# Rotating images by 90 degrees: which rows of the last group are stored first, and for which load the first store waits

## The chip, the core and the metric

The kernel runs on one core of a Trainium2 chip. It uses the vector engine (DVE), the scalar engine (ACT) and the core's 16 DMA engines; all transfers are issued from one queue, that of the sync engine (SP). The metric is the time of one execution on the device in microseconds.

## The reference

```python
batch, c, h, w = 32, 3, 256, 256                      # x is float32
np.rot90(x, k=-1, axes=(-2, -1)).astype(np.float32)
```

Each of the 96 images of 256 x 256 is turned clockwise by a quarter. Nothing is calculated: every element is read once and written once, 25.17 MB in and 25.17 MB out.

## The kernel before

**Tiles.** The input is seen as 24576 rows of 256 floats. A *slab* is 2048 rows (8 images): 128 partitions with 16 rows each, which is 16 KB per partition (`E` = 4096 floats; `Q` = 2048 is half of that, 8 rows; `W` = 256 is one row). The 12 slabs are taken in four groups of 2, 2, 4 and 4 slabs (`sizes`, L39). Each group has one tile in SBUF, `groups[n]`, called u0 to u3, which holds the whole group: it is loaded there, turned in place with the help of some spare tiles, and stored from there. So all tiles are in SBUF at once, no tile is used twice, and no load waits for a store.

**Loads** (L55 to L69). All are issued on SP's queue at the start, in the order of the groups. For the groups 1 to 3 the load `i` of `I` fills every `I`-th partition (`to[i::I]`), in two halves per partition (`a`). In the last group a half is 32 KB, that is two slabs, and a load covers 32 partitions. The last load of all is issued as two: the first half (L66, 1 MB, kept as `mark`) and the second half (L67, 1 MB).

**The turn.** DVE transposes blocks of 32 x 32 (`turn`, L82), and strided patterns on both sides put every element at its place. For a group of four slabs the work is cut in eight: two halves `t`, and four quadrants, A to D, by the halves (`low`, `high`) of the rows and columns. A transposition `move(t, c, r)` (L107) writes into all four slabs of its tile, in the other half `t`; with `c = low` it writes into the lower 8 rows (the lower 8 KB) of each slab's 16, with `c = high` into the upper 8. Two of the eight parts have to be kept aside first: ACT copies one in (L157), DVE transposes the other into the tiles `most` and `rest` (`leave`, L161 and L162). The order of the last group is: the moves D, C and B for both `t` (L164 to L166), ACT's copies of the kept part into the slabs 0, 2, 1, 3 (`enter`, L167 to L170), and last of all DVE's transposition of the part kept by ACT (L171), which writes with `c = low` and `r = low`.

**Order.** `keep` (L73) fixes the order of the instructions on DVE and on ACT as written. The waits between engines and transfers are not written out; the framework derives them from which parts of a tile each instruction and each transfer reads and writes.

**Stores** (L174 to L190). Also on SP's queue, in the order of the groups. Each group is stored in two parts, the even and the odd partitions (`a::2`, 64 partitions each); of each slab a partition's 16 KB go to 16 KB of the output. The very first store is told to wait for `mark` (L178), so that stores do not go into the queue ahead of the loads. In the last group the even partitions are stored in three pieces: slab 0's upper 8 KB, slab 0's lower 8 KB (both L189, 512 KB each), and then the slabs 1 to 3 (L190, 3 MB); the odd partitions follow in one piece of 4 MB (L190).

Of the kernel before, what the change touches and what calls it, by code (L numbers as in the profile page):

```python
# [9 lines left out]
def kernel(  # L10
# [14 lines left out]
    nc = tc.nc  # L25
    fp32 = mybir.dt.float32

    B, C, H, W = x.shape
    P = nc.NUM_PARTITIONS
    R = 16  # L30
    E = R * W
    Q = E // 2
# [8 lines left out]
    groups = [  # L41
        ctx.enter_context(tc.tile_pool(name=f"group{n}", bufs=1)).tile([P, s, E], fp32, name=f"u{n}")
        for n, s in enumerate(sizes)
    ]
# [6 lines left out]
    def rows_of(rows, n):  # L51
        return rows[first[n] * P * R : (first[n] + sizes[n]) * P * R]


    ld = rows_of(rows_in, 0).rearrange("(s i p r) w -> s i p (r w)", s=2, i=2, p=P)  # L55
# [4 lines left out]
    for n in range(1, len(sizes)):  # L60
        I = sizes[n]
        ld = rows_of(rows_in, n).rearrange("(a i m r) w -> i m a (r w)", a=2, i=I, m=P // I)
        to = groups[n].rearrange("p s f -> p (s f)").rearrange("p (a f) -> p a f", a=2)
        for i in range(I):
            if (n, i) == (len(sizes) - 1, I - 1):
                mark = nc.sync.dma_start(out=to[i::I, 0], in_=ld[i][:, 0])  # L66
                nc.sync.dma_start(out=to[i::I, 1], in_=ld[i][:, 1])  # L67
            else:
                nc.sync.dma_start(out=to[i::I], in_=ld[i])  # L69
# [61 lines left out]
    u = groups[0]  # L131
# [42 lines left out]
    st = rows_of(rows_out, 0).rearrange("(s i m r) w -> i m s (r w)", s=2, i=2, m=P // 2)  # L174
# [5 lines left out]
    for n in range(1, len(sizes)):  # L180
        I = sizes[n]
        st = rows_of(rows_out, n).rearrange("(a i m r) w -> a m i (r w)", a=2, i=I, m=P // 2)
        for a in range(2):
            done = 0
            if (n, a) == (len(sizes) - 1, 0):

                done = 1
                for f in (slice(Q, E), slice(0, Q)):
                    nc.sync.dma_start(out=st[a][:, 0, f], in_=groups[n][a::2, 0, f])  # L189
            nc.sync.dma_start(out=st[a][:, done:], in_=groups[n][a::2, done:])  # L190


# [28 lines left out]
```

## Time and profile before

| | |
|---|---|
| Median of 3 runs | 123.51 us (123.16 to 123.54) |
| The profiled execution's own time | 123.7 us |
| Its span in the profile | 121.9 us |
| DVE busy | 86.6 us, 71% of the span |
| ACT busy | 29.1 us, 24% |
| DMA queue | 50.33 MB, 97.2% of 16 engines' span |
| First store issued | at 59.40 us |
| Last transposition of the last group | 96.03 to 99.64 us |
| First store of the last group issued | at 99.71 us |

Positions in time count from the start of the span. A transfer has an issue (the time that SP's queue needs to hand it over) and, later, its packets on the 16 DMA engines; each DMA engine works through its packets in the order in which they were issued. In the profile, an issue row has the issue alone; GB/s and the DMA share come from the packets, each counted where it starts. A packet of 16 KB takes 0.61 us on its engine, so in windows of a quarter of a microsecond the rate jumps; an empty stretch of more than 0.6 us is an idle queue all the same.

### The profile page before, as it was taken

Reading aid. Unit: us, or ns where it says so; the run is one execution under the profiler, and the core shown is the slowest. Engines: PE = TensorE matmul, PEld = TensorE weight load, DVE = VectorE, ACT = ScalarE, POOL = GpSimd, SP = SyncE. Lnnn points to the kernel's source line nnn. Section 1 sums busy time; section 2 is a strip of 40 time slices with the busy share of each in tenths; the row PEclk is TensorE's granted clock in tenths of the full one; section 3 lists DMA queues with packets and bytes.
Section 4 is the critical chain, followed back from the end, with each engine's and each line's share of the span. In section 5 each row is a group of like instructions: output and inputs, shape, how many; then the busy total and the mean of one; then the engine's idle time right before and its main releaser. Section 6 shows DMA issues by size and latency. Waiting matters only on the chain.

```text
span 121.9 us, 135 instructions
## 1 busy us (share of the span) xinstructions
DVE 86.6 (71%) x25; ACT 29.1 (24%) x20; POOL 0.2 (0%) x4
## 2 busy tenths in 40 slices
DVE  0039999999994199999999999999999960000000
ACT  0000400470005199409462194000003400000000
POOL 0000000000000000000000000000000000000000
DMA  3999999997979898989899999999999989999994
GB/s 86 427 430 427 435 430 430 430 516 344 516 344 516 355 505 376 484 387 473 382 430 430 419 425 414 425 430 430 430 430 430 430 344 430 430 425 425 430 430 183
DMA packets 3264, 50.33 MB, mean 413 GB/s; under 512 B 384, under 2 KB 384, under 8 KB 384
## 3 DMA queue, kind: packets, MB, share of 16 engines
q1 hardware_dynamic: 3264, 50.33, 97.2%
HBM read 25.17 MB, written 25.17 MB: 413 GB/s over the span
## 4 chain that ended last, share of the span: by engine, by line
DVE 44%; DMA 34%; issue 3%; DVEq 0%
DMA u<-in_x_dram 34%; DVE u L82 34%; DVE spare L82 6%; DVE most L82 3%; DVE extra L82 2%; DVEq L82 0%
## 5 line engine op out<-in xcount | busy, mean ns | idle before, releaser
L82 DVE STREAM_TRANSPOSE u<-u 128x2048 f32<-128x2048 f32 x16 | 59.7, 3811 | 0.3
L82 DVE STREAM_TRANSPOSE spare<-u 128x2048 f32<-128x2048 f32 (+1 forms) x4 | 11.9, 2995 | 12.7 <-DMA u<-in_x_dram 12.7
L85 ACT COPY u<-spare 128x512 f32<-128x512 f32 (+2 forms) x8 | 10.5, 1347 | 18.6 <-DVE u L82 13.8
L85 ACT COPY u<-extra 128x1024 f32<-128x1024 f32 (+1 forms) x3 | 5.7, 1937 | 11.1 <-DVE u L82 11.1
L85 ACT COPY u<-most 128x448 f32<-128x448 f32 x4 | 2.1, 563 | 20.4 <-DVE u L82 20.4
L85 ACT COPY spare<-u 128x1024 f32<-128x1024 f32 (+1 forms) x3 | 5.7, 1887 | 2.6 <-DMA u<-in_x_dram 2.6
L85 ACT COPY extra<-u 128x2048 f32<-128x2048 f32 x1 | 4.2, 4234 | 2.5 <-issue 2.5
L85 ACT ACT_TABLE_LOAD x1 | 1.3, 1283 | 13.1 <-DMA u<-in_x_dram 13.1
L82 DVE STREAM_TRANSPOSE extra<-u 128x2048 f32<-128x2048 f32 x1 | 3.9, 3920 | 0.0
L82 DVE STREAM_TRANSPOSE most<-u 128x1792 f32<-128x1792 f32 x1 | 3.6, 3634 | 0.0
L82 DVE STREAM_TRANSPOSE u<-spare 128x2048 f32<-128x2048 f32 x1 | 3.6, 3607 | 0.0
L82 DVE STREAM_TRANSPOSE spare<-spare 128x2048 f32<-128x2048 f32 x1 | 2.3, 2330 | 0.0
L82 DVE STREAM_TRANSPOSE extra<-extra 128x2048 f32<-128x2048 f32 x1 | 2.3, 2311 | 0.0
L205 POOL MEMSET const-bfloat16-1.0<- 128x1 bf16 x1 | 0.1, 101 | 0.0
L205 POOL MEMSET const-uint8-127<- 128x1 uint8 x1 | 0.1, 101 | 0.0
L205 POOL MEMSET const-float32-0.0<- 128x1 f32 x1 | 0.1, 98 | 0.2 <-issue 0.2
L205 POOL MEMSET const-float32-1.0<- 128x1 f32 x1 | 0.1, 98 | 0.0
## 6 DMA issues: line engine op xcount, KB each, us to landing
u<-in_x_dram SPq DMA_DIRECT2D x10, 2048.0 KB, 30.4
out_dram<-u SPq DMA_DIRECT2D x3, 4096.0 KB, 19.4
out_dram<-u SPq DMA_DIRECT2D x4, 2048.0 KB, 13.3
u<-in_x_dram SPq DMA_DIRECT2D x4, 1024.0 KB, 20.4
out_dram<-u SPq DMA_DIRECT2D x1, 3072.0 KB, 10.5
out_dram<-u SPq DMA_DIRECT2D x2, 512.0 KB, 3.3
```

The costliest lines, as they stand in the source:

```text
L82: keep(nc.vector.transpose(out=out, in_=in_))
L85: keep(nc.scalar.copy(out=out, in_=in_))
L205: nc = _bacc.Bacc("TRN2", target_bir_lowering=False, num_devices=1)
```

## The change

```diff
         for i in range(I):
             if (n, i) == (len(sizes) - 1, I - 1):
-                mark = nc.sync.dma_start(out=to[i::I, 0], in_=ld[i][:, 0])
+                part = I * E // 2 * 11 // 16
+                mark = nc.sync.dma_start(out=to[i::I, 0, :part], in_=ld[i][:, 0, :part])
+                nc.sync.dma_start(out=to[i::I, 0, part:], in_=ld[i][:, 0, part:])
                 nc.sync.dma_start(out=to[i::I, 1], in_=ld[i][:, 1])
...
         for a in range(2):
-            done = 0
+            u = groups[n][a::2]
             if (n, a) == (len(sizes) - 1, 0):
 
-                done = 1
-                for f in (slice(Q, E), slice(0, Q)):
-                    nc.sync.dma_start(out=st[a][:, 0, f], in_=groups[n][a::2, 0, f])
-            nc.sync.dma_start(out=st[a][:, done:], in_=groups[n][a::2, done:])
+                end = Q + 2 * W
+                nc.sync.dma_start(out=st[a][:, I - 1, end:], in_=u[:, I - 1, end:])
+                nc.sync.dma_start(out=st[a][:, : I - 1], in_=u[:, : I - 1])
+                nc.sync.dma_start(out=st[a][:, I - 1, :end], in_=u[:, I - 1, :end])
+            else:
+                nc.sync.dma_start(out=st[a], in_=u)
```

The change has two parts. The first half of the last load, 32 KB in each of 32 partitions, is issued as two loads, of 22 KB (704 KB in all) and 10 KB (320 KB); `mark`, for which the first store waits, is the one of 22 KB. And the even partitions of the last group are stored in three other pieces: first the upper 6 KB (rows 10 to 15) of slab 3, 384 KB; then the slabs 0 to 2, 3 MB; then the lower 10 KB of slab 3, 640 KB. The odd partitions follow in one piece of 4 MB as before. DVE's and ACT's instructions are the same.

## The prediction

> **What bounds the kernel now.** I read the page's slices first, then the DMA issues, then what the sync queue (SP) waited for, then the last 30 us in order of time, then quarter-microsecond windows. The slices say that the transfers are the bound:
>
> ```profile
> DVE  0039999999994199999999999999999960000000
> ACT  0000400470005199409462194000003400000000
> ...
> DMA  3999999997979898989899999999999989999994
> GB/s 86 427 430 427 435 430 430 430 516 344 516 344 516 355 505 376 484 387 473 382 430 430 419 425 414 425 430 430 430 430 430 430 344 430 430 425 425 430 430 183
> ...
> q1 hardware_dynamic: 3264, 50.33, 97.2%
> ```
>
> Each slice is 3.05 us. DVE has nothing left after slice 33, and DMA is at 8 or 9 tenths all along: 50.33 MB at 430 GB/s are 117.0 of the 121.9 us. (516 beside 344 is an effect of long packets, counted where they start; such a pair has the usual mean.) One slice stands alone: number 33, from 97.5 to 100.6 us, at 344 GB/s between two of 430. The page's chain of waits stops at DVE's last transposition, because stores are all that follows; so the end has to be followed in the transfers themselves. There the next two views matter, the order of time and the windows (DMA share and GB/s are the last two columns):
>
> ```profile
> 88.62 7.37 DVE L82 STREAM_TRANSPOSE u<-u 128x2048 f32<-128x2048 f32 x2
> 92.28 1.03 ACT L85 COPY u<-most 128x448 f32<-128x448 f32 x2 [17.64 <-DVE u L82]
> 96.03 3.61 DVE L82 STREAM_TRANSPOSE u<-spare 128x2048 f32<-128x2048 f32 x1
> 96.03 1.03 ACT L85 COPY u<-most 128x448 f32<-128x448 f32 x2 [2.71 <-DVE u L82]
> ...
> 99.71 1.13 SPq L189 DMA_DIRECT2D out_dram<-u  x2
> 100.89 1.99 SPq L190 DMA_DIRECT2D out_dram<-u  x2
> ```
>
> ```profile
> 99.50:99.75 0.25, 0.13 (x1) 0.00 (x0) 0.00 (x0) 1.00 1.39 590
> 99.75:100.00 0.25, 0.00 (x0) 0.00 (x0) 0.00 (x0) 1.00 0.00 0
> 100.00:100.25 0.25, 0.00 (x0) 0.00 (x0) 0.00 (x0) 1.00 0.04 0
> 100.25:100.50 0.25, 0.00 (x0) 0.00 (x0) 0.00 (x0) 1.00 0.00 0
> 100.50:100.75 0.25, 0.00 (x0) 0.00 (x0) 0.00 (x0) 1.00 0.00 0
> 100.75:101.00 0.25, 0.00 (x0) 0.00 (x0) 0.00 (x0) 1.00 1.18 492
> ```
>
> The last group's first store is issued at 99.71, when the last transposition is over. The stores of the group before run out meanwhile. In the trace's packet records their last packets end between 100.05 and 100.25 on the 16 DMA engines, and the first packets of the last group begin between 100.86 and 101.01: 0.78 us of idle time as the mean of 16. No other stretch has an idle engine for over 0.13 us between 1.8 us (first data) and 120.6 (last). So the gap is all that an ordering of transfers can win; it is 0.6% of the time.
>
> **The change, part by part.** *The 6 KB.* SP waits before L189:
>
> ```profile
> SPq L189 <- DVE u L82: 22.9, 1, 22.9
> SPq L216 <- DMA out_dram<-u: 18.0, 3, 9.7
> ```
>
> That wait ended with the last transposition. It writes only the lower 8 KB (low `c`) of each slab's 16 KB; the upper 8 KB were done at 95.99 (88.62 + 7.37). So in the kernel before, the upper half of slab 0 was held 3.7 us for nothing: what orders the waits takes the strided write too coarsely. In floats of a partition, that write begins at 24 (slab 0) and ends at 14335 (slab 3, row 7); the upper half of slab 0, 2048 to 4095, lies between its ends. The 6 KB of the change are 14848 to 16383, behind its last element. If spans decide, the new store waits for 95.99 only, or for ACT's copies (done at 97.32). Both are before 100.05 by more than 2 us.
>
> Then the sum is this. 6 KB from 64 partitions are 384 KB, 24 KB per DMA engine; a 16 KB packet took 0.614 us, so they last 0.92 us and the engines run dry at 100.97 to 101.17, mean 101.06. The next store (three slabs, 3 MB) can be issued at 99.71, as the first one was. The store issued then took 0.49 us to issue and its first packet came 1.15 us after the start of the issue, 0.66 after its end. The same 3 MB shape took 0.72 us to issue at 100.89. Counted from the end of the issue, its first packet comes at 99.71 + 0.72 + 0.66 = 101.09; from the start, at 100.86. What is left of the gap is 0.12 us at most, some 0.04 as a mean. The gain is 0.78 - 0.04 = 0.74. The 10 KB piece and the last 4 MB are issued behind it while 3 MB (7.3 us) run, so even the slow issues of the trace (1.2 to 1.4 us) are covered there.
>
> *The count and size of pieces.* Stores: 10 before and 10 after, with as many runs (64 + 64 + 192 in the first half of the group). Loads: 14 become 15. Two more packets per engine: 8 KB took 0.309 us and 16 KB 0.614, so a cut costs 2 x 0.309 - 0.614 = 0.004 us, twice, and one more completion record of 0.009. Together 0.02 us, on the path, since the queue is the bound. Runs of 6, 10 and 22 KB are not in the trace. From below they cost nothing; from above, the slowest 8 KB packets (0.345 where 0.309 is usual, 12%) on the 2 MB concerned, 4.9 us, would cost 0.6 us. I take nothing: 8 KB and 16 KB rows differ by 1%.
>
> Here a rule of the Trainium skill speaks against cutting. "DMA: Bandwidth & Descriptors", section Bandwidth, asks for 1 MiB or more per transfer, and its section Anatomy of one DMA (written for another issuing path than this kernel's) puts a fixed 2.0 us on each; charged to the one added piece, that would be an estimated 125.5 us. The trace's two 512 KB stores of L189 follow one another at 1.25 us each, 420 GB/s, with the queue fed, so the row decides against that charge; a store into an empty queue does pay, and that is the gap.
>
> *The hold.* The first store now waits for 22 KB per partition of the last load's first half, not 32: 20 KB per engine fewer, 0.77 us. It would be issued at 58.63 instead of 59.40. Does it help? Its first packets came at 60.876, within 0.01 us of the end of the last load's (60.87 to 61.24): there is no gap to close. Issue end plus 0.66 gives 60.74, a margin of 0.13 us, which grows to 0.90. I count zero; it could be worth 0.1 in executions where the margin is lost. A loss would have to come from stores that wait in the queues beside loads; from 60.9 to 63.3, where one follows the other, the rate is 430 GB/s, so I bound it at 0.1 too. Eight DMA semaphores are used in turn, so each issue waits for the DMA eight places before it; the added load moves all later ones by a place. The second half's load is issued one 2 MB load later (4.9 us; 32.6 instead of 27.7), with loads queued until 60.9. Who reads the last group waits for one more semaphore, about 0.05 us on DVE, which first reads that group at 69.77, 8 us after the last load lands; ACT's copies then waited 2.6 us for the last half, whose landing does not move. Behind the held store SP has nothing but stores.
>
> **Sum.** 0.74 - 0.02 = 0.72. The profiled execution took 123.7 us (span 121.9 and 1.8 around it), so 122.98; it lies 0.19 above the median of the runs shown. On the median: 123.51 - 0.72 = 122.79, forecast 122.8.
>
> **Rivals.** (1) *The 6 KB do not leave early.* For: the wait before L189 is coarse, and another wait is coarser than my span reading: ACT's copy of the last group's slab 0 waited for the load of slabs 2 and 3, which lies behind everything that it reads:
>
> ```profile
> ACT spare L85 <- DMA u<-in_x_dram: 2.6, 1, 2.6
> ```
>
> There, too, one side is a DMA over stepped partitions. Against: slabs are told apart elsewhere. The first transposition began at 8.19, though the load of the other slab of its tile landed at 13.08; ACT's copies into slabs 0 and 2 went at 92.28, those into 1 and 3 at 96.03, each with the transposition that reads that slab. If the wait stays at 99.64, the gap stays too: 6 KB at 100.86, dry at 101.78, and the 3 MB store, issued at 100.25, has its first packet at 100.25 + 0.72 + 0.66 = 101.63. Then 123.51 + 0.02 = 123.5: no change.
>
> (2) *The same, and a second gap: slower.* Before, a small store (0.54 us to issue) followed the first 8 KB. Now 3 MB follow 6 KB. If that issue takes as long as the 4 MB ones behind another store (1.40 and 1.22), its first packet comes at 100.25 + 1.40 + 0.66 = 102.31, 0.53 after the engines ran dry: 123.51 + 0.53 + 0.02 = 124.1. It decides from an issue of 0.87 us on. Against: the one row of that shape is 0.72.
>
> (3) *Early, but with a slow issue.* The 6 KB leave at 96, and the 3 MB issue takes 1.40: first packet at 101.77, dry at 101.06, 0.71 idle in place of 0.78. Then 123.5. Against: issues after SP's long waits took 0.60 and 0.68.
>
> **Chances.** Forecast 0.56, unchanged wait (1) 0.27, (2) 0.11, (3) 0.06. A difference of 0.3%, 0.37 us, is about what a measurement of this kernel can tell from no change. Faster by more than that: 0.56, from the forecast. Slower by more: (2) and the odd runs' cost, 0.13. Within: 0.31. The range goes from 122.6 (the gap gone wholly, and the 0.1 of the hold) to 123.65 (case 1 and 0.1 for noise); what it leaves out is case 2 and a part of the odd runs, under 0.2. The forecast's own range is 122.6 to 123.1.
>
> **What would show it.** Right: SP's wait for DVE before the first store of the last group shrinks from 22.9 to about 19.3 us, its issue stands near 96 or 97, the quarter-microsecond windows from 99.75 to 100.75 carry data, slice 33 reads 430. The first store is issued near 58.6 and nothing else follows from it. Wrong: an issue at 99.7 (case 1), a 3 MB issue over 0.87 us with empty windows near 102 (case 2) or 101 (case 3), or 6 and 10 KB packets slower than 26 GB/s per engine.

## The result, and the profile after

The changed kernel takes 122.78 us (median of 6 runs, 122.65 to 122.91); the kernel before, with the runs beside it, 123.21 us (6 runs, 123.16 to 123.54). The ratio is 0.9957, with a 95% interval of 0.9945 to 0.997: a gain of 0.53 us, between 0.37 and 0.68. The forecast was 122.8, from a gain of 0.72 on a median of 123.51. The time agrees better than its parts do, and that is partly luck: the gain was forecast too large (0.43 us between the medians, where 0.72 was forecast), from a starting point that further runs put 0.3 lower, and the two errors cancel.

The page of the changed kernel; its own execution took 122.8 us, the span is 121.0:

```profile
DVE  0029999999995099999999999999999970000000
...
DMA  3999999998989898989989999999999999999994
GB/s 84 406 433 433 463 433 433 433 509 357 498 368 498 368 498 368 487 379 412 455 379 428 433 433 433 433 433 428 433 433 433 433 420 447 433 407 443 428 433 173
...
q1 hardware_dynamic: 3312, 50.33, 97.6%
```

Slice 33 reads 420 where it read 344: the lone low slice has gone. What SP waited for, the longest first:

```profile
SPq L178 <- DMA u<-in_x_dram: 25.5, 1, 25.5
SPq L190 <- DVE u L84: 19.2, 1, 19.2
...
SPq L191 <- DVE u L84: 3.1, 1, 3.1
```

The 22.9 us before the last group's first store have become 19.2 and 3.1: the 6 KB store (L190) is released by the transposition before the last, the 3 MB (L191) by the last one. In the order of time:

```profile
84.52 10.98 DVE L84 STREAM_TRANSPOSE u<-u 128x2048 f32<-128x2048 f32 x3
...
95.53 0.49 SPq L190 DMA_DIRECT2D out_dram<-u  x1
...
95.53 3.60 DVE L84 STREAM_TRANSPOSE u<-spare 128x2048 f32<-128x2048 f32 x1
...
99.20 0.60 SPq L191 DMA_DIRECT2D out_dram<-u  x1
99.85 0.61 SPq L192 DMA_DIRECT2D out_dram<-u  x1
100.52 1.32 SPq L194 DMA_DIRECT2D out_dram<-u  x1
```

The 6 KB are issued at the same moment as the last transposition starts, 3.7 us before the 3 MB. The 3 MB issue took 0.60 us. The windows where the queue used to be empty:

```profile
99.50:99.75 0.25, 0.00 (x0) 0.00 (x0) 0.00 (x0) 1.00 0.52 221
99.75:100.00 0.25, 0.00 (x0) 0.00 (x0) 0.00 (x0) 1.00 0.42 172
100.00:100.25 0.25, 0.00 (x0) 0.00 (x0) 0.00 (x0) 1.00 1.08 443
100.25:100.50 0.25, 0.00 (x0) 0.00 (x0) 0.00 (x0) 1.00 1.06 442
100.50:100.75 0.25, 0.00 (x0) 0.00 (x0) 0.00 (x0) 1.00 1.40 590
```

No window is empty. In the packet records there is no idle time between 98 and 106 us (0.00 us per engine), where it was 0.78.

The two profiles differ by 0.9 us of span, more than the kernels do by their ratio. The profiled execution of before (123.7 us) took longer than all six runs of that kernel, and a second profile of the same kernel shows where.

### The profile page after: what moved, and what is told of

The parts are those of the page before. It is cut to its first block, busy times and chain, and to the rows that moved or that the text cites. A ratio compares the mean times of both kernels' runs of the same rounds, so it can differ in the third digit from the quotient of the medians.

```text
span 121.0 us, 137 instructions
## 1 busy us (share of the span) xinstructions
DVE 86.1 (71%) x25; ACT 28.8 (24%) x20; POOL 0.2 (0%) x4
## 4 chain that ended last, share of the span: by engine, by line
DVE 40%; DMA 32%; issue 5%; ACT 3%; DVEq 0%
DVE u L84 34%; DMA u<-in_x_dram 32%; ACT extra L87 3%; DVE most L84 3%; DVE spare L84 2%; DVE extra L84 2%; DVEq L84 0%
## 5 line engine op out<-in xcount | busy, mean ns | idle before, releaser
L84 DVE STREAM_TRANSPOSE u<-u 128x2048 f32<-128x2048 f32 x16 | 59.4, 3777 | 0.3
```

The lines of the kernel that those rows point to most:

```text
L84: keep(nc.vector.transpose(out=out, in_=in_))
```

## The experiments

Ratios are to the kernel before in runs beside each, with 95% intervals. "Idle at 100" is the mean idle time per DMA engine between 98 and 106 us (time in which fewer than 16 packets are under way, shared out over the 16 engines); "16 KB" is the mean length of the stores' 16 KB packets between 80 and 97 us, and "16 KB after" the same between 100 and 120 us; "stretch" is by how much the 32 KB load packets over 1.235 us exceed the usual 1.216, summed per engine. All four are worked out from the packet records of one profiled execution each.

| run | ratio | interval | idle at 100, us | 16 KB, ns | 16 KB after, ns | stretch, us | last transposition ends, us |
|---|---|---|---|---|---|---|---|
| before | 1 |  | 0.78 | 614.7 | 616.6 | 0 | 99.63 |
| the same again | 0.9990 | 0.9974 to 1.0006 | 0.27 | 614.5 | 616.5 | 0 | 99.13 |
| change | 0.9957 | 0.9945 to 0.9970 | 0.00 | 611.2 | 611.5 | 0 | 99.14 |
| early piece only | 0.9969 | 0.9955 to 0.9983 | 0.00 | 615.1 | 616.8 | 0 | 99.16 |
| hold only | 0.9997 | 0.9978 to 1.0015 | 0.47 | 611.9 | 616.5 | 0 | 99.22 |
| 6 KB told to wait | 0.9992 | 0.9975 to 1.0008 | 0.55 | 611.3 | 617.4 | 0 | 99.25 |
| 8 KB of slab 3 | 0.9999 | 0.9984 to 1.0014 | 0.89 | 611.3 | 617.8 | 0 | 99.60 |
| 6 KB of slab 0 | 0.9954 | 0.9937 to 0.9971 | 0.35 | 611.0 | 617.5 | 0 | 99.86 |
| 2 KB of slab 3 | 0.9983 | 0.9968 to 0.9997 | 0.13 | 611.3 | 617.5 | 0 | 99.10 |
| held by the last load | 0.9987 | 0.9971 to 1.0003 | 0.00 | 611.0 | 611.0 | 0.71 | 99.37 |
| cut load, old hold | 0.9968 | 0.9954 to 0.9982 | 0.00 | 615.1 | 616.7 | 0 | 99.49 |
| uncut, hold 2.4 us earlier | 0.9992 | 0.9975 to 1.0008 | 0.00 | 611.0 | 611.0 | 0.34 | 99.13 |
| no hold | 1.0012 | 0.9997 to 1.0027 | 0.00 | 611.0 | 611.0 | 0.74 | 99.39 |
| 6 KB of two slabs | 0.9945 | 0.9925 to 0.9965 | 0.00 | 611.0 | 612.2 | 0 | 99.22 |

**The kernel before, once more** (no edit).

> The kernel before, profiled once more. The forecast took the idle stretch in front of the last group's first store as 0.78 us, from one execution that took 123.7 us; the change gained 0.43 to 0.53. Theory A, the gap differs between executions: in one near the median of 123.2 it is some 0.4 to 0.55 us. Theory B, the gap is 0.78 in every execution and the change pays some 0.25 elsewhere: 0.78 again. Time against before under both: no difference, within 0.1%.

Its windows of an execution of 123.18 us:

```profile
99.50:99.75 0.25, 0.00 (x0) 0.00 (x0) 0.00 (x0) 1.00 1.40 590
99.75:100.00 0.25, 0.00 (x0) 0.00 (x0) 0.00 (x0) 1.00 0.00 0
100.00:100.25 0.25, 0.00 (x0) 0.00 (x0) 0.00 (x0) 1.00 0.04 0
100.25:100.50 0.25, 0.00 (x0) 0.00 (x0) 0.00 (x0) 1.00 1.18 492
```

The empty windows are two, not four, and the idle time is 0.27 us per engine, where it was 0.78. The stores of the group before ran out at the same time (100.07 to 100.23 us); the last transposition ended 0.50 us sooner (99.13 against 99.63), and the first store followed it:

```profile
95.52 3.61 DVE L82 STREAM_TRANSPOSE u<-spare 128x2048 f32<-128x2048 f32 x1
...
99.20 1.14 SPq L189 DMA_DIRECT2D out_dram<-u  x2
```

Most of that difference, 0.42 us, arose in one transposition beside ACT's copy out of PSUM: 4304 ns in the first execution, 3883 here. ACT's copy, in the first execution and here:

```profile
54.92 4.31 ACT L85 COPY u<-spare 128x2048 f32<-128x2048 f32 x1 [4.82 <-DVE spare L82]
```

```profile
54.93 3.88 ACT L85 COPY u<-spare 128x2048 f32<-128x2048 f32 x1 [4.79 <-DVE spare L82]
```

So the gap differs between executions, by when DVE ends, and theory A holds; here it is even shorter than the 0.4 to 0.55 us that the theory named. Of 35 runs of before, 21 lie between 123.0 and 123.4 and the others spread up to 124.06; 123.7 is one of these.

**The early piece alone.**

```diff
-                part = I * E // 2 * 11 // 16
-                mark = nc.sync.dma_start(out=to[i::I, 0, :part], in_=ld[i][:, 0, :part])
-                nc.sync.dma_start(out=to[i::I, 0, part:], in_=ld[i][:, 0, part:])
+                mark = nc.sync.dma_start(out=to[i::I, 0], in_=ld[i][:, 0])
```

> The 6 KB first, the last load and the hold as before. If the early piece is the whole of the gain: the same ratio to before as the change, 0.9957, within 0.15%, and no idle stretch near 100 us. If the hold brings a part: a ratio nearer to 1, 0.997 to 0.999, and an idle stretch near 60.9 us between loads and stores.

0.9969: most of the gain, 0.38 us (0.21 to 0.55), and the gap is closed. SP's wait before the 6 KB is as short as in the change:

```profile
SPq L188 <- DVE u L82: 19.3, 1, 19.3
```

There is no idle stretch between loads and stores near 60.9 us. The ratio lies 0.0012 above the change's; the intervals overlap, so by the times alone a part of the hold is neither shown nor excluded.

**The hold alone** (against the kernel before).

```diff
-                mark = nc.sync.dma_start(out=to[i::I, 0], in_=ld[i][:, 0])
+                part = I * E // 2 * 11 // 16
+                mark = nc.sync.dma_start(out=to[i::I, 0, :part], in_=ld[i][:, 0, :part])
+                nc.sync.dma_start(out=to[i::I, 0, part:], in_=ld[i][:, 0, part:])
```

> The load of 22 and 10 KB and the earlier hold, the stores as before. If the hold is worth nothing and a cut costs 0.02 us: a ratio of 1.000, within 0.1%, with the first store issued near 58.6 us instead of 59.4 and its first packets still at 60.9. If the hold brings a part of the gain: 0.997 to 0.999. If the cut load costs what is missing of the forecast gain (0.2 us): 1.002.

0.9997: nothing. The first store was issued at 58.71, and the stores ran a little faster (611.9 ns), but the queue then ran dry the sooner and waited for DVE: the idle time at 100 us is 0.47, where it was 0.27 with nearly the same end of DVE. Behind the gap the packets were as long as in the kernel before (616.5 ns). A gain ahead of the gap is swallowed by it.

**The 6 KB told to wait.** The price of the forecast's case 1.

```diff
-    turn(out=g3.dst[:, 0, low, low], in_=kept.rearrange("p a r g c -> p c r g a"))
+    final = nc.vector.transpose(out=g3.dst[:, 0, low, low], in_=kept.rearrange("p a r g c -> p c r g a"))
+    keep(final)
...
-                nc.sync.dma_start(out=st[a][:, I - 1, end:], in_=u[:, I - 1, end:])
+                piece = nc.sync.dma_start(out=st[a][:, I - 1, end:], in_=u[:, I - 1, end:])
+                tc.add_manual_dep(piece.ins, final.ins.name, mybir.DependencyInfo(
+                    mybir.DependencyClass.Sync, mybir.DependencyReason.SCHED_ONLY), reason="late")
```

> The changed kernel, except that the 6 KB store is told to wait for the last transposition. This is the forecast's case 1 with its price. If the early issue is what gains: the gap is back, 0.5 to 0.8 us, and the ratio is 1.000, within 0.15%; by case 2 a second gap of up to 0.5 us follows if the 3 MB issue takes over 0.87 us, ratio 1.004; by the row of 0.72 there is none. If the new order or sizes of the pieces gain by themselves: 0.996 to 0.998 in spite of the wait.

SP's wait before the 6 KB:

```profile
SPq L191 <- DVE u L173: 22.8, 1, 22.8
```

0.9992, no difference to before, with a gap of 0.55. The early issue is what gains, not the order or the sizes. The 3 MB issue took 0.60 us behind the small one, so the second gap of case 2 did not come.

**Eight kilobytes of slab 3, and six of slab 0.** My reason for the early leave was the span of the last write. These two runs part it from a reach of a few rows.

```diff
-                end = Q + 2 * W
+                end = Q
```

> As the change, but the first piece is the whole upper half of slab 3, rows 8 to 15, 8 KB, which the last transposition does not write. Theory S, span: a write is taken to cover all from its first element to its last (floats 24 to 14335); the piece, 14336 to 16383, lies behind it and leaves at about 96 us; ratio as the change, 0.9957. Theory R, reach: a write is taken to reach a little beyond row 7 in every slab, so rows 8 and perhaps 9 are held and rows 10 to 15 are free, whichever the slab; the piece waits for the last transposition, the gap stays; ratio 1.000.

```diff
-                nc.sync.dma_start(out=st[a][:, I - 1, end:], in_=u[:, I - 1, end:])
-                nc.sync.dma_start(out=st[a][:, : I - 1], in_=u[:, : I - 1])
-                nc.sync.dma_start(out=st[a][:, I - 1, :end], in_=u[:, I - 1, :end])
+                nc.sync.dma_start(out=st[a][:, 0, end:], in_=u[:, 0, end:])
+                nc.sync.dma_start(out=st[a][:, 1:], in_=u[:, 1:])
+                nc.sync.dma_start(out=st[a][:, 0, :end], in_=u[:, 0, :end])
```

> As the change, but the 6 KB come from slab 0 (rows 10 to 15, floats 2560 to 4095), then the slabs 1 to 3, then slab 0's lower 10 KB. Theory S, span: these lie between the first and the last element of the last write, so the piece waits for it and the gap stays; ratio 1.000. Theory R, reach: rows 10 to 15 are free in every slab, it leaves at about 96 us; ratio as the change, 0.9957.

SP's wait before the first piece, first with 8 KB of slab 3, then with 6 KB of slab 0:

```profile
SPq L190 <- DVE u L84: 23.0, 1, 23.0
```

```profile
SPq L190 <- DVE u L84: 19.5, 1, 19.5
...
SPq L191 <- DVE u L84: 3.1, 1, 3.1
```

The span theory fails in both. The 8 KB behind the last written element waited for the last transposition (ratio 0.9999); the 6 KB between its first and last elements left early, issued at 96.25 (0.9954). With the kernel before, where 8 KB of slab 0 waited, four cases agree: from row 8 on a piece waits, from row 10 on it does not, in the first slab as in the last. Whether row 8, row 9 or the piece's length decides was not tried.

The execution with slab 0 shows something else. DVE ended at 99.86, and 0.35 us of idle time stayed behind the 6 KB: they cover 0.92 us, and this gap would have been longer.

**Two kilobytes.** A third of the cover.

```diff
-                end = Q + 2 * W
+                end = E - 2 * W
```

> As the change, but the first piece is 2 KB (rows 14 and 15 of slab 3), 128 KB in all, 8 KB per DMA engine, 0.31 us of transfer where 6 KB are 0.93. It leaves early under both theories on the wait. If the gain is the transfer time laid into the gap: of a gap of 0.5 to 0.8 us 0.2 to 0.5 stay, an idle stretch behind the small piece; ratio 0.9975 to 0.9985. If any early store is enough (because the queue is then awake): as the change, 0.9957.

0.9983, between before and the change, with 0.13 us idle behind the piece. The gain goes by how much transfer lies in the gap, not by whether a store is under way.

The column "16 KB after" shows a second price of a gap. In the five profiles in which the packets were short up to 97 us and the queue then ran dry (hold only, 6 KB told to wait, 8 KB, 6 KB of slab 0, 2 KB), even for 0.13 us, they took 616.5 to 617.8 ns behind it. In the five in which they were short and it did not run dry, they took 611.0 to 612.2. Six ns on the 28 such packets of each engine are some 0.17 us (an estimate). That the dry queue makes the packets longer is not shown; the two go together in all ten.

**Held by the last load.**

```diff
-                mark = nc.sync.dma_start(out=to[i::I, 0], in_=ld[i][:, 0])
-                nc.sync.dma_start(out=to[i::I, 1], in_=ld[i][:, 1])
+                nc.sync.dma_start(out=to[i::I, 0], in_=ld[i][:, 0])
+                mark = nc.sync.dma_start(out=to[i::I, 1], in_=ld[i][:, 1])
```

(against the kernel with the early piece alone.)

> The 6 KB first; the last load in two halves as before; the first store is held by the second half, not by the first. It lands at about 61.7 us, so the first store is issued near 61.85, and its first packet comes 0.68 + 0.66 later, at 63.2, where the last load's packets end at 60.85 to 61.2. If the hold matters only by its margin to that end: a new gap of some 2.2 us, ratio 0.9957 + 0.018 = 1.014. If stores behind loads cost something and a later hold is good: less than 1.010.

This did not test what it was made for. Only the store of the even partitions is held; with so late a hold the framework put the other one first, and it was issued at 32.80, into the queues behind the loads, the held one at 62.60. The expected gap of 2.2 us could not come. But the packet records showed what no profile had shown before: the last 32 KB load packets took up to 2.08 us, 0.71 us per engine in all. And all later store packets took 611 ns. So the time of the first store's issue matters in two ways, and the next runs go after both.

**The cut with the old hold.**

```diff
-                mark = nc.sync.dma_start(out=to[i::I, 0, :part], in_=ld[i][:, 0, :part])
-                nc.sync.dma_start(out=to[i::I, 0, part:], in_=ld[i][:, 0, part:])
+                nc.sync.dma_start(out=to[i::I, 0, :part], in_=ld[i][:, 0, :part])
+                mark = nc.sync.dma_start(out=to[i::I, 0, part:], in_=ld[i][:, 0, part:])
```

> As the change, with the load cut in 22 and 10 KB, but the first store held by the 10 KB load, that is at the old time of about 59.4 us. In the profiles so far the stores' 16 KB packets took 611.0 to 611.9 ns between 80 and 97 us wherever the hold was the 22 KB load, and 614.5 to 615.1 with the old one (before, before again, early piece only); over 36 us of stores 0.5% are 0.2 us. Theory M: the earlier issue of the first store (0.9 us ahead of the end of the loads, not 0.13) makes it; then 614 to 615 here, ratio as the early piece alone, 0.997. Theory C: the cut load makes it (other packet lengths, other order among the 16 engines); then 611 to 612, ratio as the change, 0.9957. Theory N, chance of the execution: either, and e11 need not fit.

Issued at 59.55; 615.1 ns; 0.9968. As the early piece alone: the cut in itself neither gains nor costs.

**No cut, with an earlier hold.**

```diff
-                mark = nc.sync.dma_start(out=to[i::I, 0], in_=ld[i][:, 0])
+                nc.sync.dma_start(out=to[i::I, 0], in_=ld[i][:, 0])
                 nc.sync.dma_start(out=to[i::I, 1], in_=ld[i][:, 1])
             else:
-                nc.sync.dma_start(out=to[i::I], in_=ld[i])
+                mark = nc.sync.dma_start(out=to[i::I], in_=ld[i])
```

(against the kernel with the early piece alone.)

> The early 6 KB; the last load in two halves as before, not cut further; the first store held by the load before it (2 MB, landing at 56.85 us), so issued near 57.0, 2.4 us ahead of the old one. Theory M: 611 to 612 ns, ratio 0.9957. Theory C: 614 to 615 ns, ratio 0.997. If a store that stands in the queues well before the loads end stretches the last loads, as in the run with the late hold, where a store got in at 32.8 us and the last 32 KB packets took up to 2.08 us where 1.22 is usual, 0.71 us per engine in all: some of that here, a ratio up to 1.001.

Issued at 56.98; 611.0 ns, as theory M has it; but the last loads were stretched by 0.34 us, and the ratio is 0.9992.

**No hold** (the early piece alone, and the three lines of `add_manual_dep` behind the first store taken out).

> The early 6 KB; the last load in two halves as before; no hold at all, so the first stores are issued as soon as their rows are turned and their semaphores are free, from about 32.7 us. If each DMA engine just works through its queue in order: no effect, ratio 0.9957 to 0.997. If stores that stand behind the loads stretch the last loads: 0.7 us or more, ratio 1.002 to 1.005, to be seen in 32 KB packets over 1.3 us before 61 us.

The first stores' issues in this run, and then the windows around the end of the loads, here and, in the second fence, in the changed kernel:

```profile
32.63 5.42 SPq L176 DMA_DIRECT2D out_dram<-u  x2
42.32 5.41 SPq L189 DMA_DIRECT2D out_dram<-u  x2
```

```profile
59.50:60.00 0.50, 0.50 (x1) 0.00 (x0) 0.00 (x0) 1.00 3.36 918
60.00:60.50 0.50, 0.50 (x1) 0.00 (x0) 0.00 (x0) 1.00 0.26 66
60.50:61.00 0.50, 0.50 (x1) 0.00 (x0) 0.00 (x0) 1.00 0.00 0
61.00:61.50 0.50, 0.50 (x1) 0.00 (x0) 0.00 (x0) 1.00 0.47 197
```

```profile
59.50:60.00 0.50, 0.50 (x1) 0.00 (x0) 0.00 (x0) 1.00 2.12 918
60.00:60.50 0.50, 0.50 (x1) 0.00 (x0) 0.00 (x0) 1.00 0.30 131
60.50:61.00 0.50, 0.50 (x1) 0.00 (x0) 0.00 (x0) 1.00 0.31 131
61.00:61.50 0.50, 0.50 (x1) 0.00 (x0) 0.00 (x0) 1.00 1.17 492
```

Between 59.5 and 60.0 both start the same bytes (918 GB/s by start), but the packets that start there take 3.36 of share against 2.12: they are longer, and what should start next comes later. 0.74 us per engine go there, and the ratio is 1.0012, against 0.9969 with the hold: the hold is worth some 0.4%.

**Six kilobytes of two slabs.**

```diff
-                nc.sync.dma_start(out=st[a][:, I - 1, end:], in_=u[:, I - 1, end:])
-                nc.sync.dma_start(out=st[a][:, : I - 1], in_=u[:, : I - 1])
-                nc.sync.dma_start(out=st[a][:, I - 1, :end], in_=u[:, I - 1, :end])
+                nc.sync.dma_start(out=st[a][:, 2:, end:], in_=u[:, 2:, end:])
+                nc.sync.dma_start(out=st[a][:, :2], in_=u[:, :2])
+                nc.sync.dma_start(out=st[a][:, 2:, :end], in_=u[:, 2:, :end])
```

> As the change, but the early piece is rows 10 to 15 of the slabs 2 and 3, 768 KB, 1.85 us per engine, then the slabs 0 and 1, then the lower 10 KB of the slabs 2 and 3. The last transposition ended anywhere from 99.1 to 99.9 us in the profiles; with 6 KB of one slab 0.37 to 0.43 us of idle time stayed where it ended at 99.86 and 0.04 where it ended at 99.14. If that spread is what is left to win: no idle stretch whatever the execution, the upper runs of the change go, ratio 0.995, 0.0005 to 0.001 under the change. If longer pieces cost by their smaller runs: as the change or above.

0.9945 (122.81 us, 122.62 to 122.89). It is faster than before, and by 0.0012 in the ratio under the change, well inside the intervals: a better cover for a late DVE is plausible and not shown. This execution's DVE ended at 99.22, where 6 KB of one slab are enough.

## Why the prediction was right, and where it was not

*What bounds the kernel* and *the gap as the prize* were right: closing it is most of the gain (early piece alone 0.9969), and undoing only the early issue gives all of it back (0.9992, 0.9999). That the gap is *all* that an order of transfers can win was too narrow; see the hold below.

*The gap's size was mis-sized.* The sum used 0.78 us, from one execution, and forecast a gain of 0.74 for the piece. The second execution had 0.27 of idle time there, and the piece alone gained 0.38 (0.21 to 0.55). The prediction noted that its execution lay 0.19 us above the median and did not ask whether the gap was what made it so. It was, for the most part: DVE ended 0.50 us later there, and the gap ends when DVE does. The hit on 122.8 has this in it: between the medians of six runs the gain is 0.43 instead of 0.72, and the base of 123.51 was high by 0.30 (by 0.2 against the 28 to 35 runs beside the experiments, 123.29 to 123.33).

*The reason that the 6 KB leave early* was wrong, and that the outcome was right is luck: by the same reason 8 KB of slab 3 would have left early, and they waited. I argued by the span from 24 to 14335. The runs with 8 KB of slab 3 and 6 KB of slab 0 went the opposite way in both cases; the first two rows behind the written half, or the length that they add, decide. The counter-evidence that the prediction gave for rival (1), a wait of ACT's that a span could not explain, pointed the right way: the span is not the rule.

*The cover* of 0.92 us fits: 0.04 us of idle time were forecast, and none stayed in the change. But there DVE ended at 99.14, half a microsecond before the end that the sum went by, so this is no test of it; nearer is the cut load with the old hold, also without idle time, where DVE ended at 99.49. The cover does not suffice in every execution (0.35 with DVE's end at 99.86).

*The count and size of pieces* at nearly nothing was right: 6, 10 and 22 KB packets took 0.234, 0.386 and 0.840 us, 26.2, 26.6 and 26.8 GB/s per engine, against 26.8 for 16 KB; and the cut load with the old hold gave 0.9968 beside 0.9969 without the cut. No 2 us appeared for the added piece, so the trace's row was the better guide than the fixed charge of about 2 us that the Trainium skill gives for transfers issued on another path ("DMA: Bandwidth & Descriptors", section Anatomy of one DMA).

*The hold at zero* was wrong in substance. In all seven profiled kernels whose first store was issued at about 58.7, and in the three with still earlier issues, the 16 KB packets took 611.0 to 611.9 ns between 80 and 97 us; in all four with an issue at 59.4 to 59.6 they took 614.5 to 615.1. The cut plays no part in that. Only with the gap closed do the packets stay short to the end: all store packets together take 58.72 us per engine in the change and 59.14 with the early piece alone. The profiled executions differ by 0.31 us (122.80 against 123.11); the ratios (0.9957 against 0.9969 and 0.9968, 0.15 us) fit a gain but do not show it by themselves. Alone the hold gave nothing, because the gap behind it took the time back. My bound of 0.1 us for the other side, a loss, holds for the change itself, where no load packet was stretched. It would not have held for a hold 2.4 us earlier or for none: 0.34 and 0.74 us of stretch. It was read from a part of the trace in which the store was issued too late to show it.

*Rival (1)* did not occur, but its price was right where a run forced the wait: 123.5 forecast as "no change", 0.9992 and 0.9999 measured. *Rivals (2) and (3)* did not occur: the 3 MB issue took 0.60 us wherever it followed the small piece.

Still open: why a first store that is issued with only 0.13 us of margin to the loads' end goes with store packets 0.5% longer 20 to 36 us afterwards (not at once: in the second profile of the kernel before they took 611.1 ns between 62 and 75 us); why the packets are longer behind a dry queue; and why a store waiting far ahead in the queues stretches the last load packets. The first and the last were seen with the issue time alone changed, and no run here looks inside.

## What to carry to other kernels

When transfers bound a kernel, look for the one place where the queue runs dry, and lay there a transfer that is ready before the engine that everyone waits for; cover the latest arrival, not the one in the profile at hand. Measure such a gap in two executions at least, since it ends with an engine whose own time varies. A saving ahead of the gap shows only when the gap is closed as well (hold alone 0.9997), so test such parts together, and each alone.

## What the runs showed that was not expected

- Stores queued behind loads on the same DMA engines lengthen the loads' last packets: 32 KB in up to 2.37 us instead of 1.22 without a hold, 0.34 us per engine with an issue 2.4 us earlier than before, nothing with one 0.75 us earlier.
- The same 16 KB store packets take 611 or 615 ns for tens of microseconds, by when the first store was issued; and behind a stretch in which the queue ran dry they took 616 to 618 ns in all seven profiles that had one.
- A transposition on DVE and ACT's copy out of PSUM, side by side, took 4304 and 4313 ns in one execution and 3883 each in another of the same kernel; the 0.42 us went on to the end of DVE's chain.
